# Where the wide operands of a 512-token encoder block lie within 512 bytes of a partition

## The chip, the cores and the metric

The kernel runs on one core of one Trainium2 chip. The metric is the device time of one execution in microseconds (us); lower is better. Before the change it took 1190.75 us, the median of three runs (1190.05 to 1191.32).

## The reference

One layer of a streaming encoder on `x` of 512 tokens by 1024 features, all in float32: a half-step SwiGLU feed-forward network, a mixer, a second half-step feed-forward network, a last RMS norm.

```python
x = x + 0.5 * swiglu(rms_norm(x, ffn1_norm), ffn1_w1, ffn1_w3, ffn1_w2)   # 1024 -> 2816 -> 1024
h = rms_norm(x, mix_norm)
p = h @ w_in                                     # 1024 -> 5288 columns, for all that follows
y_a = rwkv7_mixer(token_shift(p[..., :SHIFT_COLS]), ...) @ rwkv_proj      # 512 -> 1024
y_b = fox_mixer(p_fox, ...) @ fox_proj                                    # 512 -> 1024
x = x + (sigmoid(gate_a) * y_a + sigmoid(gate_b) * y_b) @ w_out           # 1024 -> 1024
x = x + 0.5 * swiglu(rms_norm(x, ffn2_norm), ffn2_w1, ffn2_w3, ffn2_w2)
out = rms_norm(x, final_norm)
```

`rwkv7_mixer` is a delta-rule recurrence over time with a 64 by 64 state for each of 8 heads; `fox_mixer` is causal attention with 8 heads and a cumulative forget bias.

## The kernel before, in words

**Tiles.** Activations are held with features on the 128 partitions and the 512 tokens along the partition, so a tile of one feature block is 128 x 512 float32, 2048 bytes of each partition. Weights come in slices of `kt` blocks of 128 rows by 128 columns, 512 bytes a block.

**Wide products.** Every product with a weight matrix is done by `mm3` (L123 to L126). Each operand is split into a high part, rounded to the matmul's `fp32r` format, and a low part with the rest; three matmuls add up `whi*xhi`, `whi*xlo` and `wlo*xhi` into one PSUM bank. One matmul loads a 128x128 stationary operand and streams a moving operand of 512 columns past it. In most stages the weight slice is stationary and the activation moves; in the value product of the attention (`pv`, L832) and in the last half of the second network's down projection (`po`, L1167) it is the other way round.

**Weights.** `load_raw` (L106) issues the DMA of a slice on SyncE's queue into one of three `raw` buffers. `split_w` (L113) makes `whi` by a cast on ScalarE and `wlo` by a subtraction on VectorE, two buffers of each. So a slice's DMA waits for a `raw` buffer, a cast for a `whi` buffer, and that for the matmuls that read it.

**Stages, in order of time.** The start (L245 to L385) transposes x and does the first pair of feed-forward products (`f`) from `fraw`, `fwhi`, `fwlo` and the normed `xh`, `xl`; its order on TensorE, VectorE and ScalarE is written out by hand. `ffn` (L446) does the up products `pa` and `pb` from `xh`, `xl`, makes `hh`, `hl` from them and does the down products `pd` from those. The mixer does `pl`, `pk`, `pgt`, `pq` and `pv` from `xh`, `xl` of the second norm. The recurrence (L879) and the attention (L945) run among gate products. Then come `ppj` (L1017), first with `yh`, `yl` and `fox_proj`, then with `ya` and `rwkv_proj`, and `pw` (L1107) from `mh`, `ml` with `w_out`. The second `ffn` follows; its columns of the upper half end in `last` (L1155) as `po`, and `out` is written.

**Order.** Outside the parts ordered by hand or held by `issue_after`, a planner with modelled times chooses each engine's order of instructions while the kernel is built.

**Layout.** A pool puts its tiles one behind another in the order in which the code first asks for them, each rounded up to 32 bytes. Pools opened later lie behind earlier ones, from the left end up, or from the right end down where they have `side="right"`. `cp` (constants, L61) is the first on the left and begins at byte 16512 of a partition, which is 128 past a multiple of 512; the right end is byte 229344, 480 past a multiple of 512. The pools on the left are `cp`, `xp` (`xh`, `xl`, `acc`, `rstd`), `wp` (`raw`, `whi`, `wlo`), `tp` (temporaries and the small `mx0`, `mx1`), then by stage `x0` (the start), `hp` (`hh`, `hl`) or `rp` (`nka`, `tiny`, `omu`, `rc`, `la`, `PC`, `V4`) and `sp` (`G`, `BK`, `RD`, `Tall`, whose places `mh`, `ya`, `codes`, `ml` take over). On the right are `xr1`, then `vtp` and `t2` (`vt`, `qk`, `khi`, `klc`, whose places `yh`, `yl` take over), then `xr2`.

Of the kernel before, what the change touches and what calls it, by code (L numbers as in the profile page):

```python
# [9 lines left out]
F32 = mybir.dt.float32  # L10
F32R = mybir.dt.float32r
BF16 = mybir.dt.bfloat16
AF = mybir.ActivationFunctionType
ALU = mybir.AluOpType
# [4 lines left out]
P = 128  # L19
# [6 lines left out]
NP = DA // P  # L26
# [9 lines left out]
PAR_W0, PAR_A0, PAR_KK, PAR_KA, PAR_RK, PAR_LG, PAR_LB = 38, 42, 46, 50, 54, 58, 62  # L36
# [14 lines left out]
def kernel(  # L51
# [7 lines left out]
    dve, act, pool, pe = nc.vector, nc.scalar, nc.gpsimd, nc.tensor  # L59

    cp = ctx.enter_context(tc.tile_pool(name="cp", bufs=1))  # L61
# [8 lines left out]
    def bank(name, pool_=None):  # L70
        pool_ = pool_ or pm
        return pool_.tile([P, T], F32, tag="b", name=name)

    def tmp(name, shape=(P, T), dt=F32, tag="t", **kw):
        return tp.tile(list(shape), dt, tag=tag, name=name, **kw)


    ident = cp.tile([P, P], F32, name="ident")
    make_identity(nc, ident)
    identb = cp.tile([P, P], BF16, name="identb")  # L80
    dve.tensor_copy(identb[:], ident[:])
    ones = cp.tile([P, P], F32, name="ones")
    dve.memset(ones[:], 1.0)
    onesr = cp.tile([P, P], F32R, name="onesr")
    dve.tensor_copy(onesr[:], ones[:])
    bones = cp.tile([P, P], F32, name="bones")
    dve.memset(bones[:], 0.0)
    dve.memset(bones[0:64, 0:64], 1.0)
    dve.memset(bones[64:128, 64:128], 1.0)
    center = cp.tile([P, P], F32, name="center")  # L90
    dve.scalar_tensor_tensor(center[:], bones[:], -1.0 / 64, ident[:], op0=ALU.mult, op1=ALU.add)
    bonesr = cp.tile([P, P], F32R, name="bonesr")
    dve.tensor_copy(bonesr[:], bones[:])
    epsr = cp.tile([P, 1], F32, name="epsr")
    dve.memset(epsr[:], RMS_EPS)
    epsl = cp.tile([P, 1], F32, name="epsl")
# [23 lines left out]
    def load_w(aps, kt, n, eng=None):  # L120
        return split_w(load_raw(aps, kt, n), kt, n, eng)

    def mm3(ps, whi, wlo, xhi, xlo, first, last):  # L123
        pe.matmul(ps, whi, xhi, start=first, stop=False)  # L124
        pe.matmul(ps, whi, xlo, start=False, stop=False)  # L125
        return pe.matmul(ps, wlo, xhi, start=False, stop=last)  # L126
# [14 lines left out]
    def split(dst_hi, dst_lo, src, hi_eng="act"):  # L141
        cast = act.copy(dst_hi, src) if hi_eng == "act" else dve.tensor_copy(dst_hi, src)
        dve.tensor_tensor(dst_lo, src, dst_hi.bitcast(F32), op=ALU.subtract)
        return cast
# [2 lines left out]
        return ap.bitcast(F32)  # L147


    xctx = ExitStack()  # L150
    rtp = xctx.enter_context(tc.tile_pool(name="xr1", bufs=1, side="right"))
    xT = [rtp.tile([P, T], F32, name=f"xT{c}") for c in range(KD)]
# [64 lines left out]
    par = cp.tile([P, PAR_N], F32, name="par")  # L217

    def pc(i):
        return par[:, i:i + 1]  # L220
# [3 lines left out]
    nc.scalar.dma_start(g1[:], ffn1_norm[0].rearrange("(a b) -> a b", b=P))  # L224
    warm = bank("warm", pf)
    for _ in range(5):
        pe.matmul(warm[:, 0:P], ones[:], ones[:], start=True, stop=True)
    gtp = bank("gtp", pr)
    pe.transpose(gtp[:, 0:8], g1[:], ident[0:8, 0:8])
    dve.tensor_copy(par[:, 0:8], gtp[:, 0:8])  # L230
# [12 lines left out]
            return call  # L243

    with tc.tile_pool(name="x0", bufs=1) as x0:  # L245
        qpe, qdve, qact = Queued(pe), Queued(dve), Queued(act)
        xin = [x0.tile([P, NB, P], F32, name=f"xin{c}") for c in range(KD)]
        fraw = [x0.tile([P, KD, P], F32, name=f"fraw{i}") for i in range(2)]
# [59 lines left out]

        def fill(n):
            for _ in range(n):  # L310
                qpe.matmul(warm[:, 0:P], ones[:], ones[:], start=True, stop=True)

        turn(0)
        x_hi(0)
# [131 lines left out]
    def ffn(nrm, w1, w3, w2, nxt, during=(), first=None, final=None):  # L446
        with tc.tile_pool(name="hp", bufs=1) as hp:
            hh, hl = [], []
            def hidden(j, pa, pb):
                a = tmp("fa")  # L450
                dve.tensor_tensor(a[:], pa[:], nrm.rstd[:], op=ALU.mult)  # L451
                sa = tmp("fs")
                act.activation(sa[:], a[:], AF.Silu)
                b = tmp("fb")
                dve.tensor_tensor(b[:], pb[:], nrm.rstd[:], op=ALU.mult)  # L455
                h = tmp("fh")
                dve.tensor_tensor(h[:], b[:], sa[:], op=ALU.mult)
                hi = hp.tile([P, T], F32R, name=f"hh{j}")
                lo = hp.tile([P, T], F32R, name=f"hl{j}")
                split(hi[:], lo[:], h[:], "dve")  # L460
                hh.append(hi)
                hl.append(lo)

            summed = None
            for j in range(KF):
                c0 = j * P
                if j == 0 and first:
                    continue
                pa = bank("pa", pf if j == 1 and first else pm)
                pb = bank("pb", pr)  # L470
                for ps, w in ((pa, w1), (pb, w3)):
                    if j == 1 and first:
                        wh, wl = first[1][ps is pb]
                    else:
                        wh, wl = load_w([(0, w[0][:, c0:c0 + P])], KD, P)
                    mms = nrm.cols(ps[:], wh, wl, P, [summed] if summed else [])
                    summed = None
                    if ps is pa and nrm.rstd is None:
                        if first is None:
                            nrm.parts()  # L480
                        summed = nrm.finish(mms[-1 if first is None else -2])
                        if first:
                            hidden(0, *first[0])
                if j in during:
                    with tc.issue_after(pin.ins), tc.issue_after(loads[-1].ins):
                        during[j]()
                hidden(j, pa, pb)
            cuts = ((0, 8), (8, 8), (16, 6))

            for m in range(KD // 2 if final else KD):  # L490
                ps = bank("pd")
                for k0, kn in cuts:
                    wh, wl = load_w([(0, w2[0][k0 * P:(k0 + kn) * P, m * P:(m + 1) * P])], kn, P)
                    for k in range(k0, k0 + kn):
                        mm3(ps[:], wh[:, k - k0, :], wl[:, k - k0, :], hh[k][:], hl[k][:], k == 0, k == KF - 1)
                dve.scalar_tensor_tensor(xT[m][:], ps[:], 0.5, xT[m][:], op0=ALU.mult, op1=ALU.add)
                nxt(m)
                if final and m == 1:
                    held = final[0]()
            if final:  # L500
                final[1](hh, hl, held)
# [4 lines left out]
    def mix_add(c):  # L506
        nc.gpsimd.dma_start(xsave[c], xT[c][:])
        mix.add(c)

    ffn(nrm, ffn1_w1, ffn1_w3, ffn1_w2, mix_add, {2: load_params, 4: masks, 10: place_params}, (first, second))  # L510

    W = w_in[0]
# [5 lines left out]
    with ExitStack() as mx:  # L518
        rp = mx.enter_context(tc.tile_pool(name="rp", bufs=1))
# [11 lines left out]
        spare = [h[:, i] for h in (duo("RD2", "spare0"), duo("RD3", "spare1")) for i in range(2)]  # L531
        Tall = sp.tile([P, 2 * C * C], F32, name="Tall", tag="Tall")

        nka = rp.tile([P, NP], F32, name="nka")
        dve.tensor_scalar(nka[:], par[:, PAR_KA:PAR_KA + NP], -1.0, None, op0=ALU.mult)
        tiny = rp.tile([P, 2], F32, name="tiny")
        dve.memset(tiny[:, 0:1], 1e-24)
        dve.memset(tiny[:, 1:2], -1e-24)
        omu = rp.tile([P, PAR_W0 - PAR_MU], F32, name="omu")
# [47 lines left out]
        for o, c0, mu in ((spare[2], DA, 4), (spare[3], 0, 0)):  # L587
            ps = bank("pk")
# [3 lines left out]
        for p in range(NP):  # L592
            za.append((zslots[2 * p], zslots[2 * p + 1]))
            for i, (w_, x_, par0, o) in enumerate(((uw, lw, PAR_W0, zslots[2 * p]), (ux, lx, PAR_A0, zslots[2 * p + 1]))):
                ps = bank("pz", (pr, pf)[i])
# [421 lines left out]
        def proj(m, wt, y):  # L1017
            wh, wl = load_w([(0, wt[0][:, m * P:(m + 1) * P])], NP, P)
            ps = bank("ppj")
            for k in range(NP):  # L1020
                mm3(ps[:], wh[:, k, :], wl[:, k, :], y[k][0], y[k][1], k == 0, k == NP - 1)
            return ps
# [18 lines left out]
        for p in range(NP):  # L1041
            y = vs[p]
            yc = bank("yc", pr)
            pe.matmul(yc[:], center[:], y, start=True, stop=True)
            sq = gslot[8 + p % 2]
            act.activation(sq, yc[:], AF.Square)
            ps = bank("pg", pf)
            pe.matmul(ps[:], bones[:], sq, start=True, stop=True)
            rn = tslot[p]
            with tc.issue_after(logs.ins):  # L1050
                act.activation(rn, ps[:], AF.Ln, bias=epsl[:, 0:1], scale=1.0 / 64)
                act.activation(rn, rn, AF.Exp, scale=-0.5)
            dve.tensor_tensor(y, yc[:], rn, op=ALU.mult)
            dve.scalar_tensor_tensor(y, y, pc(PAR_LG + p), bons[p], op0=ALU.mult, op1=ALU.add)
            ps = bank("pg", pf)
            pe.matmul(ps[:], gup[0:96, p * P:(p + 1) * P], lg[0:96, :], start=True, stop=True)
            dve.tensor_tensor(y, y, ps[:], op=ALU.mult)
            parted = split(*ya[p], y)
# [7 lines left out]
        for m in range(KD):  # L1066
            g = gslot[m]
            nc.gpsimd.dma_start(g, gsave[KD + m])
            ps = proj(m, fox_proj, ybs)
# [26 lines left out]
        for m in range(KD):  # L1096
            g = slot[m]
            ps = proj(m, rwkv_proj, ya)
# [4 lines left out]
        for m in range(KD):  # L1103
            wh, wl = load_w([(0, w_out[0][:, m * P:(m + 1) * P])], KD, P)
            ps = bank("pw")
# [49 lines left out]
    def last(hh, hl, ws):  # L1155
# [20 lines left out]
        for b in range(NB):  # L1176
# [11 lines left out]
            nc.sync.dma_start(out[0, bs, HC], hi_)  # L1188

    ffn(nrm2, ffn2_w1, ffn2_w3, ffn2_w2, almost, final=(hold, last))  # L1190


# [22 lines left out]
```

## Time and profile before

| | us |
|---|---|
| median of three runs | 1190.75 |
| span of the profiled execution, from its first to its last instruction | 1188.0 |
| TensorE busy with matmuls | 1173.7 |
| TensorE busy with weight loads | 946.0 |
| VectorE busy | 657.1 |
| ScalarE busy | 459.3 |
| GpSimd busy | 87.4 |

The profile is of one execution on the chip. Its span is 2.75 us under the median time; that difference lies outside the first and last instruction. A row of a group of instructions gives line, engine, operation, output and inputs, shape, count, busy time and the mean of one. A matmul's own duration holds the time that it takes to run through the array, and the next one starts before it has ended; what a stream of matmuls costs is read from the distance of their starts, and a busy TensorE is not one at its peak.

### The profile page before, as it was taken

To read this page: it belongs to the slowest core of one execution; us is meant where nothing else is said; L and a number is where in the kernel's file an instruction comes from. 1 tells how busy PE (TensorE), PEld (TensorE's weight loads), DVE (VectorE), ACT (ScalarE), POOL (GpSimd) and SP (SyncE) were. 2 spreads that over 40 slices of the span, in tenths; PEclk is the share of its full clock that TensorE was granted. 3 is DMA by queue.
4 is the path that set the end of the run, shared out by engine and by line. 5 is a ranking of instruction groups with operands and counts; after the bars stand their busy time and mean duration, and the time that the engine had idled before them with its cause. 6 is when DMAs were issued, how large, how long until landed. Compare 5 with 4: busy or idle time off the path is not lost.

```text
span 1188.0 us, 15711 instructions
## 1 busy us (share of the span) xinstructions
PE 1173.7 (99%) x6264; PEld 946.0 (80%) x6264; DVE 657.1 (55%) x983; ACT 459.3 (39%) x746; POOL 87.4 (7%) x138
## 2 busy tenths in 40 slices
PE   9999999999999999999999999999999999999997
PEld 7888888888887888887777776778888888888886
DVE  6645554533434697786767656766545454534221
ACT  6322222222223764346786765424222222223222
POOL 1200000001111111411000020121000000000100
PEclk9999999999999999999999999999999999999999
DMA  6333333333334243344122243633333333325211
GB/s 179 111 106 90 106 89 106 89 93 104 114 116 112 78 120 112 109 140 116 37 64 88 81 132 115 211 92 97 89 106 89 103 93 105 91 87 161 89 36 71
DMA packets 201783, 122.52 MB, mean 103 GB/s; under 512 B 9934, under 2 KB 191246, under 8 KB 201710
## 3 DMA queue, kind: packets, MB, share of 16 engines
q1 hardware_dynamic: 195134, 107.62, 31.1%
q0 software_dynamic: 3760, 12.06, 3.2%
q10 hardware_dynamic: 2816, 1.84, 0.5%
q8 instruction: 49, 0.80, 0.3%
q14 instruction: 24, 0.20, 0.1%
HBM read 110.82 MB, written 10.68 MB: 102 GB/s over the span
## 4 chain that ended last, share of the span: by engine, by line
PE 92%; DVE 3%; ACT 3%; DMA 1%; issue 1%; SPq 0%; ACTq 0%; DVEq 0%
PE pb L126 7%; PE pa L126 7%; PE pa L125 7%; PE pb L125 7%; PE pb L124 7%; PE pa L124 7%; PE pd L126 5%; PE pd L124 5%; PE pd L125 5%; PE pgt L124 3%; PE pgt L125 2%; PE pgt L126 2%; PE pk L124 2%; PE pk L125 2%; PE pk L126 2%; PE po L124 2%
## 5 line engine op out<-in xcount | busy, mean ns | idle before, releaser
L116 ACT CAST whi<-raw 128x1024 fp32r<-128x1024 f32 (+3 forms) x193 | 192.7, 999 | 592.0 <-PE pa L125 177.8
L117 DVE TENSOR_TENSOR wlo<-raw,whi 128x1024 fp32r<-128x1024 f32 (+3 forms) x193 | 224.3, 1162 | 125.1 <-ACT whi L116 125.0
L126 PE MATMUL pb<-xh,wlo 128*128 128x512 f32 x344 | 133.9, 389 | 0.0
L126 PE MATMUL pa<-xh,wlo 128*128 128x512 f32 x344 | 133.9, 389 | 0.0
L125 PE MATMUL pa<-xl,whi 128*128 128x512 f32 x344 | 133.9, 389 | 0.0
L124 PE MATMUL pb<-xh,whi 128*128 128x512 f32 x344 | 133.9, 389 | 0.0
L125 PE MATMUL pb<-xl,whi 128*128 128x512 f32 x344 | 133.9, 389 | 0.0
L124 PE MATMUL pa<-xh,whi 128*128 128x512 f32 x344 | 133.9, 389 | 0.0
L455 DVE TENSOR_TENSOR fb<-pb,rstd 128x512 f32<-128x512 f32 x43 | 29.7, 691 | 139.5 <-PE pb L126 139.5
L126 PE MATMUL pd<-hh,wlo 128*128 128x512 f32 x264 | 104.6, 396 | 0.0
L125 PE MATMUL pd<-hl,whi 128*128 128x512 f32 x264 | 104.2, 395 | 0.0
L124 PE MATMUL pd<-hh,whi 128*128 128x512 f32 x264 | 104.2, 395 | 0.0
L126 PEld LDWEIGHTS pb<-xh,wlo 128*128 128x128 f32 x344 | 64.5, 188 | 13.7 <-DVE wlo L241 0.5
L125 PEld LDWEIGHTS pb<-xl,whi 128*128 128x128 f32 x344 | 64.6, 188 | 13.5
L124 PEld LDWEIGHTS pb<-xh,whi 128*128 128x128 f32 x344 | 64.6, 188 | 13.5
L126 PEld LDWEIGHTS pa<-xh,wlo 128*128 128x128 f32 x344 | 64.6, 188 | 13.4
L125 PEld LDWEIGHTS pa<-xl,whi 128*128 128x128 f32 x344 | 64.5, 188 | 13.5
L124 PEld LDWEIGHTS pa<-xh,whi 128*128 128x128 f32 x344 | 64.6, 188 | 13.4
L451 DVE TENSOR_TENSOR fa<-pa,rstd 128x512 f32<-128x512 f32 x43 | 29.7, 691 | 70.2 <-PE pa L126 70.2
L126 PEld LDWEIGHTS pd<-hh,wlo 128*128 128x128 f32 x264 | 49.6, 188 | 12.3 <-DVE wlo L117 0.5
L125 PEld LDWEIGHTS pd<-hl,whi 128*128 128x128 f32 x264 | 49.6, 188 | 11.9
L124 PEld LDWEIGHTS pd<-hh,whi 128*128 128x128 f32 x264 | 49.6, 188 | 11.8
(397 smaller groups left out, 2031.1 us busy)
## 6 DMA issues: line engine op xcount, KB each, us to landing
raw<-in_ffn_w_dram SPq DMA_DIRECT2D x121, 512.0 KB
raw<-in_w_in_dram SPq DMA_DIRECT2D x40, 512.0 KB
raw<-in_ffn_w_dram SPq DMA_DIRECT2D x12, 384.0 KB
raw<-in_w_out_dram SPq DMA_DIRECT2D x8, 512.0 KB
gsave<-gs SPq DMA_DIRECT2D x9, 256.0 KB
xin<-in_x_dram SPq DMA_DIRECT2D x8, 256.0 KB
xsave<-xT POOLq DMA_DIRECT2D x8, 256.0 KB, 2.3
G<-gsave POOLq DMA_DIRECT2D x8, 256.0 KB, 3.0
```

The costliest lines, as they stand in the source:

```text
L116: (hi_eng or act).copy(hi[:], raw[:])
L117: (eng or dve).tensor_tensor(lo[:], raw[:], hi[:].bitcast(F32), op=ALU.subtract)
L124: pe.matmul(ps, whi, xhi, start=first, stop=False)
L125: pe.matmul(ps, whi, xlo, start=False, stop=False)
L126: return pe.matmul(ps, wlo, xhi, start=False, stop=last)
L451: dve.tensor_tensor(a[:], pa[:], nrm.rstd[:], op=ALU.mult)
L455: dve.tensor_tensor(b[:], pb[:], nrm.rstd[:], op=ALU.mult)
```

## The change

No instruction of the products is changed. Two constant matrices that were kept twice, once as float32 and once as `fp32r` (`ones`, `bones`), are kept once and read through either type, which takes 1024 bytes a partition and two casts away. Four unused or merged tiles shift what lies behind them: 192 bytes at the right end (`edge`), 384 bytes ahead of the start's tiles (`lead0`), 384 bytes ahead of `hh` and `hl` (`lead`), and `nka` and `tiny` in one tile in place of two, 32 bytes less.

```diff
-    ones = cp.tile([P, P], F32, name="ones")
-    dve.memset(ones[:], 1.0)
     onesr = cp.tile([P, P], F32R, name="onesr")
-    dve.tensor_copy(onesr[:], ones[:])
-    bones = cp.tile([P, P], F32, name="bones")
-    dve.memset(bones[:], 0.0)
+    ones = onesr[:].bitcast(F32)
+    dve.memset(ones, 1.0)
+    bonesr = cp.tile([P, P], F32R, name="bonesr")
+    bones = bonesr[:].bitcast(F32)
+    dve.memset(bones, 0.0)
     dve.memset(bones[0:64, 0:64], 1.0)
     dve.memset(bones[64:128, 64:128], 1.0)
     center = cp.tile([P, P], F32, name="center")
-    dve.scalar_tensor_tensor(center[:], bones[:], -1.0 / 64, ident[:], op0=ALU.mult, op1=ALU.add)
-    bonesr = cp.tile([P, P], F32R, name="bonesr")
-    dve.tensor_copy(bonesr[:], bones[:])
+    dve.scalar_tensor_tensor(center[:], bones, -1.0 / 64, ident[:], op0=ALU.mult, op1=ALU.add)
...
+    edge = ctx.enter_context(tc.tile_pool(name="edge", bufs=1, side="right"))
+    edge.tile([P, 48], F32, name="edge")
     xctx = ExitStack()
     rtp = xctx.enter_context(tc.tile_pool(name="xr1", bufs=1, side="right"))
...
     with tc.tile_pool(name="x0", bufs=1) as x0:
+        x0.tile([P, 96], F32, name="lead0")
...
         with tc.tile_pool(name="hp", bufs=1) as hp:
             hh, hl = [], []
+            hp.tile([P, 96], F32, name="lead")
+
...
-        nka = rp.tile([P, NP], F32, name="nka")
-        dve.tensor_scalar(nka[:], par[:, PAR_KA:PAR_KA + NP], -1.0, None, op0=ALU.mult)
-        tiny = rp.tile([P, 2], F32, name="tiny")
+        small = rp.tile([P, NP + 2], F32, name="small")
+        nka, tiny = small[:, 0:NP], small[:, NP:NP + 2]
+        dve.tensor_scalar(nka, par[:, PAR_KA:PAR_KA + NP], -1.0, None, op0=ALU.mult)
```

The other lines of the diff drop a `[:]` where `ones` and `bones` are used (L227, L311, L1048).

More of the change, by code (lines that the diff above doesn't have):

```diff
@@ L226 @@
     for _ in range(5):
-        pe.matmul(warm[:, 0:P], ones[:], ones[:], start=True, stop=True)
+        pe.matmul(warm[:, 0:P], ones, ones, start=True, stop=True)
     gtp = bank("gtp", pr)
@@ L310, in fill @@
             for _ in range(n):
-                qpe.matmul(warm[:, 0:P], ones[:], ones[:], start=True, stop=True)
+                qpe.matmul(warm[:, 0:P], ones, ones, start=True, stop=True)
         turn(0)
@@ L1047 @@
             ps = bank("pg", pf)
-            pe.matmul(ps[:], bones[:], sq, start=True, stop=True)
+            pe.matmul(ps[:], bones, sq, start=True, stop=True)
             rn = tslot[p]
```

## The prediction

> **What bounds the kernel now.** I read the profile's page first: busy times, the chain that ended last, then the groups.
>
> ```profile
> span 1188.0 us, 15711 instructions
> PE 1173.7 (99%) x6264; PEld 946.0 (80%) x6264; DVE 657.1 (55%) x983; ACT 459.3 (39%) x746; POOL 87.4 (7%) x138
> ...
> PEclk9999999999999999999999999999999999999999
> ...
> PE 92%; DVE 3%; ACT 3%; DMA 1%; issue 1%; SPq 0%; ACTq 0%; DVEq 0%
> ...
> L126 PE MATMUL pb<-xh,wlo 128*128 128x512 f32 x344 | 133.9, 389 | 0.0
> L126 PE MATMUL pd<-hh,wlo 128*128 128x512 f32 x264 | 104.6, 396 | 0.0
> ```
>
> TensorE is the bound: 92% of the chain is its matmuls, at a granted clock of 0.9 or more in every slice. So the time is the number of matmuls times the distance of their starts, and the groups hint that this is not the same everywhere: `pb` matmuls last 389 ns, `pd` matmuls of the same shape 396 ns. To get the distance itself I took stretches in which one product ran without a break. The columns are the stretch, its length, then busy time and count (x) for TensorE's matmuls and its weight loads, then other engines, granted clock, DMA share and GB/s. The first and fourth rows count every instruction, the others those of `pd`, `po` and `ppj` alone.
>
> ```profile
> 60.00:240.00 180.00, 180.00 (x796) 148.97 (x796) 89.55 (x116) 44.84 (x50) 0.00 (x0) 1.00 0.34 99
> ...
> 256.00:372.00 116.00, 116.00 (x499) 93.31 (x498) 4.84 (x7) 1.00 0.37 108
> ...
> 1132.00:1180.00 48.00, 48.00 (x208) 38.90 (x208) 2.08 (x3) 1.00 0.15 54
> ...
> 524.00:544.00 20.00, 20.00 (x90) 16.57 (x89) 16.66 (x37) 7.39 (x12) 2.60 (x7) 1.00 0.41 122
> ...
> 744.20:754.30 10.10, 10.10 (x45) 8.13 (x44) 2.20 (x4) 1.00 0.96 316
> ```
>
> A matmul under way at the left edge is counted too, so the distance is the length plus one duration (0.39 us), over the count. For `pa` and `pb` (first row) 180.39/796 = 226.6 ns; for `pq` (fourth) 20.39/90 = 226.6; for `pd` 116.39/499 = 233.3; for `po` 48.39/208 = 232.7; for `ppj` 10.49/45 = 233.1. For `pw` I use the first and the last of 28 rows in a stretch of the timeline (start, duration):
>
> ```profile
> 767.31 0.40 PE L124 MATMUL pw<-mh,whi 128*128 128x512 f32 x1
> ...
> 773.61 0.39 PE L124 MATMUL pw<-mh,whi 128*128 128x512 f32 x1
> ```
>
> That is 6.30/27 = 233.3 ns. All five rows show a clock of 1.00, and the DMA shares of `pa` (0.34) and `pd` (0.37) are alike, so neither explains 226.6 against 233.
>
> **What the layout says.** I worked out where each operand starts, mod 512 bytes, from the order and size of the declared tiles. `cp` starts at 128 and holds 4256 bytes, so `xp`, `wp` and the large temporaries lie at 288: `xh`, `xl`, `whi`, `wlo`. Behind them stand four 32-byte tiles (`mx0`, `mx1`), so `hh`, `hl` and the start's `fwhi`, `fwlo` lie at 416. In the mixer 160 bytes of small tiles, `la` (2048) and 256 of `PC` follow instead: 416+160+256 = 832, or 320, for `V4`, `ya`, `mh`, `ml`, `codes`. The right end and all of 2048 bytes under it lie at 480: `yh`, `yl`, `uw`, `ux`. So both operands of `pa`, `pb`, `pk`, `pgt`, `pq`, `pv` are at 288, and those are the products at 226.6 ns. The ones near 233 pair 416 with 288 (`pd`, and with the roles swapped `po`, `f`), 320 with 288 (`ppj`, `pw`), 480 with 288 (`ppj`). Neither a moving operand at 288 (`po` has it) nor a stationary one at 288 (`pd` has it) is enough; both have to agree.
>
> One product tests this apart from the stage and the region of memory. `pl` has `xh` and `whi` at 288 like `pk`, but its weight slice has 72 or 96 columns, so the blocks of a slice stand 288 or 384 bytes apart and most start elsewhere mod 512. First and last of 24 rows each:
>
> ```profile
> 374.48 0.39 PE L124 MATMUL pl<-xh,whi 128*72 128x512 f32 x1
> ...
> 379.80 0.39 PE L126 MATMUL pl<-xh,wlo 128*72 128x512 f32 x1
> ...
> 380.49 0.40 PE L124 MATMUL pl<-xh,whi 128*96 128x512 f32 x1
> ...
> 385.80 0.40 PE L126 MATMUL pl<-xh,wlo 128*96 128x512 f32 x1
> ```
>
> 5.32/23 = 231.3 ns and 5.31/23 = 230.9: not 226.6, though the weights are narrower. And the step comes at once where `pb` hands over to `pd`, with no wait between:
>
> ```profile
> 250.83 0.39 PE L125 MATMUL pb<-xl,whi 128*128 128x512 f32 x1
> 251.06 0.39 PE L126 MATMUL pb<-xh,wlo 128*128 128x512 f32 x1
> 251.29 0.40 PE L124 MATMUL pd<-hh,whi 128*128 128x512 f32 x1
> ```
>
> **The change, part by part.** *Addresses.* Two 512-byte constants go, 1024 bytes, which is 0 mod 512: `xh` and `whi` stay at 288. `lead` and `lead0` add 384: `hh`, `hl`, `fwhi`, `fwlo` go to 416+384 = 800, or 288. `small` saves 32: `V4` and all behind it go to 288. `edge` takes 192 off the right: `yh`, `yl` go to 288. So `f`, `pd`, `po`, `pw` and `ppj` all become 288 with 288. I take the 226.6 ns of the stretches that are so today. The counts are 3 matmuls for each block of weights:
>
> - `pd`: 3 x 264 = 792 matmuls by 233.3-226.6 = 6.7 ns: 5.31 us.
> - `po`: 4 token blocks x 22 x 3 = 264 by 6.1 ns: 1.61 us.
> - `pw`: 8 x 8 x 3 = 192 by 6.7 ns: 1.29 us.
> - `ppj`: 2 x 8 x 4 x 3 = 192 by 6.5 ns: 1.25 us.
> - `f`: 48. Eighteen of them took 4.20 us (below), 233.3 each; broken by transposes they may not all settle, so 0.15 to 0.32 us; I take 0.2.
>
> Sum 9.66 us. Now what of it is not collected. While `ppj` reads `ya` the DMA engines are 0.96 busy at 316 GB/s, and TensorE runs out of weights once:
>
> ```profile
> 744.97 10.01 DMA raw<-in_rwkv_proj_dram
> 755.08 0.63 ACT whi L116
> 755.75 0.50 PE ppj L124
> ...
> PE ppj L124 <- ACT whi L116: 1.0, 1, 1.0
> ```
>
> The slice was issued at 744.97, and its landing at 755 is set by the DMA engines, not by matmuls: the 48 between give 48 x 6.5 = 0.31 us that only lengthens this wait. In `pd` of the second network, where `hold` loads extra slices, a weight load waited 0.5 us for `wlo`; I take up to 0.3 us off there:
>
> ```profile
> PEld pd L126 <- DVE wlo L117: 0.5, 1, 0.5
> ACT whi L116 <- PE pd L125: 132.5, 34, 5.1
> ```
>
> The second row says that everywhere else in `pd` ScalarE waits for matmuls to free `whi`, 34 times, up to 5.1 us: weights stand ready, and `pa`, with the same 512 KB for 24 matmuls, is fed at 226.6 already. So 9.66-0.31-0.3 = 9.05 us, say 9.0.
>
> *Casts that go.* The start's chain, below, runs through SyncE's queue, a weight DMA, a cast and `f`; VectorE's two casts (0.72 and 0.23 us) lie before 2.7 us beside the 5.32 us DMA. They give nothing, and without that cover at most 0.95 us.
>
> ```profile
> 1.16 0.72 DVE L85 CAST onesr<-ones 128x128 fp32r<-128x128 f32 x1
> 2.44 0.23 DVE L93 CAST bonesr<-bones 128x128 fp32r<-128x128 f32 x1
> ...
> 1.86 5.32 DMA fraw<-in_ffn_w_dram
> 7.20 0.63 ACT fwhi L241
> 7.87 1.71 PE f L241 x6
> ...
> 17.78 4.20 PE f L241 x18
> ```
>
> *Merged `nka` and `tiny`.* The same three VectorE operations in the same order; no wait is added, no DMA and no queue. *Other pairs.* `pz` (8 matmuls, 320 with 480) becomes equal; `pn` (16: `khi` goes from 416 to 224 against `bonesr` at 384) and eight attention products against `qb0` (64 to 32, `klc` 480 to 288) stay unequal. At 6.7 ns either way, 32 matmuls are bounded by 0.2 us; I take 0. *VectorE, ScalarE and DMA* also read and write at moved places; the cast into `fwhi` at 416 took 0.63 us, that into `whi` at 288 the same 0.63 (rows above), so 0.
>
> The profiled span would be 1188.0-9.0 = 1179.0; 2.75 us outside it remain, so 1181.75.
>
> **The rivals.** *The offset is not the cause (no change).* The streams near 233 ns all have one operand above the temporaries, in the start's, the network's or the mixer's own pools, those at 226.6 have both below; the region could be it. Against it stands `pl`, both operands below and at 231. The time would be 1190.75. The Trainium skill speaks for this rival: "SBUF — State Buffer", section "Who interferes with whom", gives TensorE two independent read ports, one for the moving operand and one for weight loads, and says that TensorE never waits on anyone, by which the relative offset could cost nothing. The two distances above do not agree with it as far as it would mean one distance for all. That the padding lands elsewhere than I count belongs to this rival too. Chance 7%.
>
> *Only part settles.* Shift of phase, not the final place, makes the gain, and only unbroken streams keep it: `pd` of the first network (528) gains 3.5 us, the stages with waits, transposes or hand-overs half of their 5.5: 6.3 in all, 1184.5. If those gain nothing, 1187.2. For it: `pl` reads 231 even with some blocks equal. Against: `pq` shows 226.6 in a stretch with 37 VectorE instructions beside it. Chance 12%.
>
> *Slower: the planner re-orders the recurrence.* With two casts fewer its modelled times shift, and instruction order may change where no hand wrote it. The place is the recurrence, where TensorE was busy 162.49 of 167 us and waits on copies:
>
> ```profile
> 545.00:712.00 167.00, 162.49 (x1632) 125.26 (x1631) 114.05 (x244) 121.52 (x303) 8.75 (x16) 0.99 0.29 82
> 568.13 1.24 DVE wlo L117
> PE sps L901 <- ACT RD L896: 2.5, 3, 1.5
> ```
>
> A `wlo` subtraction (1.24 us) put ahead of the state update delays it and TensorE behind it. Over all 16 steps that is 19.8 us: 1190.75-9.0+19.8 = 1201.6. It decides from eight steps on (8 x 1.24 = 9.9). Against: the casts are over before 3 us, behind them stand hand-ordered operations, and SyncE's weights come later anyway. Chance 6%.
>
> **How the numbers follow.** Forecast 75%: 1181.75, its own range 1179.8 to 1183.5: below, nothing lost (9.66), the other pairs' 0.2, half of the casts' 0.95 and 0.6 for the spread of the runs; above, a loss three times as large and the same spread. Part settles 12%, no change 7%, slower 6%. To leave out no more than two in ten the range runs to 1185.5 and takes in half of the second case. About 0.2% (2.4 us) is what a measurement of this kernel can tell from no change: faster 0.87, same 0.07, slower 0.06.
>
> **What would show it.** In the changed profile `pd`, `po`, `pw`, `ppj` stand at about 389 ns a matmul and 226.6 from start to start, `pl` stays near 231, `pa` unchanged; `ppj` still waits once for weights near 745 to 755 less some 4 us, and its wait is 0.3 longer; the recurrence keeps its length. If the distances fall to 226.6 and the time does not, a wait has taken the gain: look in the stretch 700 to 780. If they stay at 233, the offset is not the cause.

## The result and the profile after

| | median us | runs | lowest to highest |
|---|---|---|---|
| before | 1190.40 | 4 | 1189.70 to 1191.32 |
| after | 1182.72 | 4 | 1181.52 to 1183.46 |

The ratio is 0.9935, with a 95% interval of 0.9923 to 0.9947: 6.3 to 9.2 us of 1190.4. The forecast was 1181.75. The profiled execution took 1182.64 us with a span of 1180.9, so that of the 9.05 us that the forecast took off the span 1188.0, 7.1 came.

The page of the changed kernel, the lines that answer to those of before (casts are now L114 and L115, `mm3` is L122 to L124):

```profile
span 1180.9 us, 15709 instructions
PE 1165.0 (99%) x6264; PEld 945.6 (80%) x6264; DVE 656.3 (56%) x981; ACT 459.5 (39%) x746; POOL 87.4 (7%) x138
...
PE 91%; ACT 3%; DVE 3%; DMA 2%; issue 1%; SPq 0%; ACTq 0%; DVEq 0%
...
L124 PE MATMUL pb<-xh,wlo 128*128 128x512 f32 x344 | 133.9, 389 | 0.1
...
L124 PE MATMUL pd<-hh,wlo 128*128 128x512 f32 x264 | 103.1, 391 | 0.5 <-DVE wlo L115 0.5
```

As many matmuls as before, and still the bound; those of `pd` now last 389 to 391 ns, no longer 396. The distances come from the same kind of stretch as before (stretch, length, then busy time and count of TensorE's matmuls, its weight loads and so on; the first and the last row count every instruction, the others those of `pd`, `po` and `ppj` alone):

```profile
60.00:240.00 180.00, 180.00 (x797) 148.96 (x796) 89.53 (x116) 44.84 (x50) 0.00 (x0) 1.00 0.34 98
...
256.00:368.00 112.00, 112.00 (x496) 92.75 (x495) 4.84 (x7) 1.00 0.39 112
...
1128.00:1174.00 46.00, 46.00 (x204) 37.91 (x202) 2.07 (x3) 1.00 0.13 46
...
740.50:750.30 9.80, 9.80 (x45) 8.10 (x44) 2.25 (x4) 1.00 0.96 322
...
545.00:712.00 167.00, 162.30 (x1628) 124.61 (x1627) 112.15 (x242) 122.27 (x303) 8.73 (x16) 0.99 0.29 84
```

`pa` and `pb` stay at 180.39/797 = 226.3 ns (226.6 before). `pd` has come down to 112.39/496 = 226.6 (from 233.3), `po` to 46.39/204 = 227.4 (from 232.7), `ppj` to 10.19/45 = 226.4 (from 233.1). TensorE's busy time in the recurrence's 167 us is 162.30 beside 162.49: nothing has moved there. Where `pb` hands over to `pd` the distance no longer rises. The three rows that the prediction shows of that place, 0.23 us apart on both sides, are too few to tell 226.6 from 233 ns at 0.01 us; the first and the 25th row of `pd` do tell them (timeline, start and duration; before, then changed):

```profile
251.29 0.40 PE L124 MATMUL pd<-hh,whi 128*128 128x512 f32 x1
...
256.88 0.40 PE L124 MATMUL pd<-hh,whi 128*128 128x512 f32 x1
```

```profile
251.33 0.39 PE L122 MATMUL pd<-hh,whi 128*128 128x512 f32 x1
...
256.77 0.39 PE L122 MATMUL pd<-hh,whi 128*128 128x512 f32 x1
```

That is 5.59/24 = 232.9 ns before and 5.44/24 = 226.7 now.

The one place that the forecast marked as a loser is the wait for the first slice of `rwkv_proj`. In the chain of waits of the changed kernel, and in the timeline of TensorE with the idle time in brackets:

```profile
741.32 10.47 DMA raw<-in_rwkv_proj_dram
751.88 0.63 ACT whi L114
752.55 0.50 PE ppj L122
...
750.47 0.39 PE L124 MATMUL ppj<-ya,wlo 128*128 128x512 f32 x1
752.55 0.50 PE L122 MATMUL ppj<-ya,whi 128*128 128x512 f32 x1 [1.69 <-ACT whi L114]
```

Before, the same wait was 1.0 us. The `ppj` matmuls from `ya` ahead of it gained 0.27 us, and the transfer took 10.47 us in place of 10.01: 0.27 + 0.46 is the whole of the longer wait (the gap between the two starts is 2.08 us, it was 1.36).

Where the 7.1 us arose is read from the starts of the stages' first and last matmuls in both timelines. The gain of a stage is the difference of its own length:

| stage | forecast us | measured us |
|---|---|---|
| start, up to the first `pa` (21.82 in both) and to the first `pd` | 0.2 | -0.04 |
| `pd` of the first network | 3.54 | 3.51 |
| up to `ppj`, with the recurrence | 0 | -0.13 |
| `ppj`, with its wait | 0.94 | 0.13 |
| `pw` | 1.29 | 1.17 |
| up products of the second network | 0 | 0.03 |
| `pd` of the second network, with its wait | 1.47 | 0.95 |
| `po` | 1.61 | 1.41 |
| sum | 9.05 | 7.03 |

The one long run of products without an interruption, `pd` of the first network, paid as worked out; the two stages with a wait for weights fell short, `ppj` by nearly all of its gain.

### The profile page after: what moved, and what is told of

It is laid out like the page before. It is cut to its first block, busy times and chain, and to the rows that moved or that the text cites. A ratio compares the mean times of both kernels' runs of the same rounds, so it can differ in the third digit from the quotient of the medians.

```text
span 1180.9 us, 15709 instructions
## 1 busy us (share of the span) xinstructions
PE 1165.0 (99%) x6264; PEld 945.6 (80%) x6264; DVE 656.3 (56%) x981; ACT 459.5 (39%) x746; POOL 87.4 (7%) x138
## 4 chain that ended last, share of the span: by engine, by line
PE 91%; ACT 3%; DVE 3%; DMA 2%; issue 1%; SPq 0%; ACTq 0%; DVEq 0%
PE pb L124 7%; PE pb L122 7%; PE pb L123 7%; PE pa L124 6%; PE pa L122 6%; PE pa L123 6%; PE pd L124 5%; PE pd L123 5%; PE pd L122 5%; PE pgt L122 3%; PE pgt L124 2%; PE pgt L123 2%; PE pk L123 2%; PE pk L122 2%; PE pk L124 2%; PE po L122 2%
## 5 line engine op out<-in xcount | busy, mean ns | idle before, releaser
L114 ACT CAST whi<-raw 128x1024 fp32r<-128x1024 f32 (+3 forms) x193 | 192.8, 1000 | 586.1 <-PE pa L123 177.8
L115 DVE TENSOR_TENSOR wlo<-raw,whi 128x1024 fp32r<-128x1024 f32 (+3 forms) x193 | 224.2, 1162 | 122.8 <-ACT whi L114 122.7
L124 PE MATMUL pb<-xh,wlo 128*128 128x512 f32 x344 | 133.9, 389 | 0.1
L124 PE MATMUL pa<-xh,wlo 128*128 128x512 f32 x344 | 133.9, 389 | 0.0
L122 PE MATMUL pb<-xh,whi 128*128 128x512 f32 x344 | 133.8, 389 | 0.0
L123 PE MATMUL pb<-xl,whi 128*128 128x512 f32 x344 | 133.8, 389 | 0.0
L123 PE MATMUL pa<-xl,whi 128*128 128x512 f32 x344 | 133.8, 389 | 0.0
L122 PE MATMUL pa<-xh,whi 128*128 128x512 f32 x344 | 133.8, 389 | 0.0
L124 PE MATMUL pd<-hh,wlo 128*128 128x512 f32 x264 | 103.1, 391 | 0.5 <-DVE wlo L115 0.5
L122 PE MATMUL pd<-hh,whi 128*128 128x512 f32 x264 | 102.8, 389 | 0.0
L123 PE MATMUL pd<-hl,whi 128*128 128x512 f32 x264 | 102.8, 389 | 0.0
L124 PEld LDWEIGHTS pb<-xh,wlo 128*128 128x128 f32 x344 | 64.5, 188 | 13.9 <-DVE wlo L241 0.6
L124 PEld LDWEIGHTS pa<-xh,wlo 128*128 128x128 f32 x344 | 64.6, 188 | 13.5
L123 PEld LDWEIGHTS pb<-xl,whi 128*128 128x128 f32 x344 | 64.6, 188 | 13.5
L123 PEld LDWEIGHTS pa<-xl,whi 128*128 128x128 f32 x344 | 64.5, 188 | 13.5
L122 PEld LDWEIGHTS pb<-xh,whi 128*128 128x128 f32 x344 | 64.6, 188 | 13.3
L122 PEld LDWEIGHTS pa<-xh,whi 128*128 128x128 f32 x344 | 64.6, 188 | 13.3
L124 PEld LDWEIGHTS pd<-hh,wlo 128*128 128x128 f32 x264 | 49.6, 188 | 11.1 <-DVE wlo L115 0.9
L123 PEld LDWEIGHTS pd<-hl,whi 128*128 128x128 f32 x264 | 49.6, 188 | 10.4
L122 PEld LDWEIGHTS pd<-hh,whi 128*128 128x128 f32 x264 | 49.6, 188 | 10.2
```

The lines of the kernel that those rows point to most:

```text
L114: (hi_eng or act).copy(hi[:], raw[:])
L115: (eng or dve).tensor_tensor(lo[:], raw[:], hi[:].bitcast(F32), op=ALU.subtract)
```

## The experiments

The theory: a 128x512 matmul starts 226.6 ns after the one ahead of it if both operands lie at one offset mod 512, and 233 if not, wherever they are. Its rivals: the gain comes from the casts or from another order of instructions; from the region or the absolute place; from a smaller condition than one offset mod 512. Every edit is against the changed kernel.

**Without the lead of `hh` and `hl`** (`pd` and `po` back at 416 with 288; the rest of the change stays).

```diff
             hh, hl = [], []
-            hp.tile([P, 96], F32, name="lead")
```

> The changed kernel without the 384 bytes ahead of hh and hl: these lie at 416 again, all other operands stay at 288. If the distance of the two operands mod 512 sets the pace, pd of both networks and po go back to about 233 ns from start to start and give back what they gained in the traces (3.5 + 0.9 + 1.4 us), so about 5.9 us more than the changed kernel, some 1188.6 us, with pw and ppj still at 226.6. If the region of memory, the dropped casts or the planner made the gain, the time stays at 1182.7.

Measured: 1188.92 us, ratio to before 0.9990 (0.9981 to 0.9999). Stretches of `pd` and of `po` in this kernel:

```profile
260.00:366.00 106.00, 106.00 (x456) 85.27 (x455) 4.84 (x7) 1.00 0.37 110
...
1130.00:1172.00 42.00, 42.00 (x183) 34.04 (x182) 1.51 (x3) 1.00 0.15 51
```

`pd` is at 106.39/456 = 233.3 ns again, `po` at 42.39/183 = 231.6. By the spans of the profiled executions (1186.9 beside 1180.9) some 6 of the 7 us hang on this one unused tile of 384 bytes.

**The constants alone** (`edge`, `lead0`, `lead` out, `nka` and `tiny` apart again; the two constant matrices stay merged).

```diff
-    edge.tile([P, 48], F32, name="edge")
...
-        x0.tile([P, 96], F32, name="lead0")
...
-            hp.tile([P, 96], F32, name="lead")
...
-        small = rp.tile([P, NP + 2], F32, name="small")
-        nka, tiny = small[:, 0:NP], small[:, NP:NP + 2]
...
+        nka = rp.tile([P, NP], F32, name="nka")
...
+        tiny = rp.tile([P, 2], F32, name="tiny")
```

> Only the constants are kept once; no padding, nka and tiny apart, so all operands have the offsets of the kernel before (1024 bytes less is 0 mod 512). Offset theory: the time of the kernel before, 1190.4, within 0.5 us, and every distance as before. If dropping two casts or the planner's new order helped, part of the 7.7 us appears here.

Measured: 1190.34 us, ratio 1.0003 (0.9994 to 1.0013). The casts that went and any shift of modelled times bring nothing that can be told; all of the gain lies in the places.

**Everything 32 bytes on** (all wide operands at 320).

```diff
+    cp.tile([P, 8], F32, name="shift")
...
-    edge.tile([P, 48], F32, name="edge")
+    edge.tile([P, 40], F32, name="edge")
```

> The changed kernel with everything moved on together by 32 bytes: all operands of the wide products at 320 in place of 288. If only their distance counts: 226.6 ns everywhere and 1182.7 us. If 288 itself is a good place, or a multiple of 64 or 128 a bad one: all 4500 wide matmuls near 233 ns, 20 us and more added.

Measured: 1182.69 us, ratio 0.9935 (0.9919 to 0.9952), as the changed kernel. The same stretch of `pd`:

```profile
260.00:366.00 106.00, 106.00 (x469) 87.76 (x468) 4.84 (x7) 1.00 0.39 114
```

106.39/469 = 226.8 ns. 288 is no special place; only the relation of the operands counts.

**128 bytes between `xp` and `wp`** (`xh`, `xl` stay at 288, the weights and all other wide operands go to 416). Now the products that were short in both kernels have unequal operands, and `pd`, `pw`, `ppj` equal ones. So has `po`, but for eight of its 22 blocks of weights (`ownh`, `ownl`): these are held in the places of `xh` and `xl`, at 288, and meet `hh`, `hl` at 416.

```diff
+    gap = ctx.enter_context(tc.tile_pool(name="gap", bufs=1))
+    gap.tile([P, 32], F32, name="gap")
...
-    edge.tile([P, 48], F32, name="edge")
+    edge.tile([P, 16], F32, name="edge")
```

> 128 bytes between the activations' pool and the weights' pool: xh and xl at 288, weights and all other operands at 416. Offset theory: pa and pb (2064 matmuls) go from 226.6 to about 233 ns, 13.8 us; pk, pgt, pq and pv (960) likewise where TensorE is the bound, 3 to 6.4 us; pd, po, pw and ppj stay at 226.6 because both of theirs are at 416. So 1199.5 to 1203 us. If both operands have to be at 288, pd, po, pw and ppj go back to 233 too: about 1208 to 1211. If the offsets do nothing: 1182.7.

Measured: 1200.53 us, ratio 1.0083 (1.0068 to 1.0098). First the stretch of `pa` and `pb`, then that of `pd`:

```profile
60.00:240.00 180.00, 180.00 (x775) 145.19 (x774) 87.67 (x114) 43.28 (x48) 0.00 (x0) 1.00 0.33 96
...
260.00:366.00 106.00, 106.00 (x470) 87.76 (x468) 4.84 (x7) 1.00 0.39 112
```

`pa` and `pb` now stand at 180.39/775 = 232.8 ns, `pd` at 106.39/470 = 226.4. Within `po` the eight blocks at 288 are long, 21 rows of which the first and last are

```profile
1158.69 0.40 PE L124 MATMUL po<-ownh,hh 128*128 128x512 f32 x1
...
1163.35 0.40 PE L126 MATMUL po<-ownh,hl 128*128 128x512 f32 x1
```

or 4.66/20 = 233.0 ns, while its steps with weights at 416 average 227.4. An unused 128 bytes cost 17.8 us against the changed kernel: `pa` and `pb` have 3 x 2 x 344 = 2064 matmuls and the mixer's products from `xh`, without `pl`, another 960 (40 slices of 24), at 6.2 ns each 18.7 us. This is the strongest evidence, since the effect was put where it had never been. It is also the test of the rule in the Trainium skill, page "SBUF — State Buffer", section "Who interferes with whom", that the moving operand and the weight loads have independent read ports and TensorE waits for nobody: as far as that would mean that their relative place costs nothing, this run does not agree.

**Small distances** (`hh` and `hl` 4 bytes from the weights in the first network, 16 in the second, `ya`, `mh`, `ml` 64, `yh`, `yl` 256).

```diff
+            hall = hp.tile([P, 2 * KF * T + 8], F32R, name="hall")
+            at = 4 if final else 1
...
-                hi = hp.tile([P, T], F32R, name=f"hh{j}")
-                lo = hp.tile([P, T], F32R, name=f"hl{j}")
+                hi, lo = [hall[:, at + i * T:at + (i + 1) * T] for i in (2 * j, 2 * j + 1)]
...
-        small = rp.tile([P, NP + 2], F32, name="small")
+        small = rp.tile([P, NP + 18], F32, name="small")
...
-    edge.tile([P, 48], F32, name="edge")
+    edge.tile([P, 112], F32, name="edge")
```

> The changed kernel with other distances between activation and weights, mod 512 bytes: 4 in pd of the first network, 16 in pd and po of the second, 64 in ppj with ya and in pw, 256 in ppj with yh; pa, pb and the mixer's input products stay equal. If the two have to agree to the byte: all these streams near 233 ns, pa at 226.6, and the time of the kernel before, 1189.5 to 1190.5 us. If only the coarse part of the address counts (lines of 32 or 64 bytes): pd and po keep 226.6 and some 5.9 us of the gain, about 1184.5 us.

**Large distances** (`hh`, `hl` 256 in the first network, -32 in the second, `ya`, `mh`, `ml` 96, `yh`, `yl` -64).

```diff
-            hp.tile([P, 96], F32, name="lead")
+            hp.tile([P, 88 if final else 160], F32, name="lead")
...
-        small = rp.tile([P, NP + 2], F32, name="small")
+        small = rp.tile([P, NP + 26], F32, name="small")
...
-    edge.tile([P, 48], F32, name="edge")
+    edge.tile([P, 64], F32, name="edge")
```

> As before with distances of 256 in pd of the first network, 32 less in pd and po of the second, 96 in ppj with ya and in pw, 64 less in ppj with yh. Agreement mod 512 needed: all near 233 ns and 1189.5 to 1190.5 us. If 256 is as good as 512: pd of the first network stays at 226.6 and keeps 3.5 us, about 1186.5 us. If one of these distances gives less than 226.6 ns, it would be a better place than the change's.

Measured: 1191.81 us, ratio 1.0012 (1.0003 to 1.0021), for the small ones; 1187.30, ratio 0.9975 (0.9964 to 0.9985), for the large ones. From the small distances, `pd` at 4 bytes, `po` at 16, `pw` at 64:

```profile
260.00:366.00 106.00, 106.00 (x447) 84.48 (x446) 4.85 (x7) 1.00 0.37 109
...
1130.00:1172.00 42.00, 42.00 (x182) 34.01 (x181) 1.38 (x2) 1.00 0.15 51
...
786.00:808.00 22.00, 22.00 (x98) 18.06 (x97) 2.77 (x4) 1.00 0.35 103
```

From the large ones, `pd` at 256, `po` at -32, `pw` at 96, and the first and last of 25 rows of `ppj` from `yh`, `yl` at -64:

```profile
256.00:368.00 112.00, 112.00 (x496) 92.75 (x495) 4.84 (x7) 1.00 0.39 112
...
1130.00:1172.00 42.00, 42.00 (x182) 33.74 (x181) 2.08 (x3) 1.00 0.13 47
...
786.00:808.00 22.00, 22.00 (x96) 17.69 (x95) 2.77 (x4) 1.00 0.33 97
...
733.64 0.40 PE L124 MATMUL ppj<-yh,wlo 128*128 128x512 f32 x1
...
739.24 0.40 PE L124 MATMUL ppj<-yh,wlo 128*128 128x512 f32 x1
```

| distance of activation from weights, bytes | ns from start to start |
|---|---|
| -64 (`ppj` from `yh`) | 5.60/24 = 233.3 |
| -32 (`po`) | 42.39/182 = 232.9 |
| 4 (`pd`) | 106.39/447 = 238.0 |
| 16 (`po`) | 42.39/182 = 232.9 |
| 64 (`pw`) | 22.39/98 = 228.5 |
| 96 (`pw`) | 22.39/96 = 233.2 |
| 128 (`pa`, `pb`) | 232.8 |
| 256 (`pd`) | 112.39/496 = 226.6 |

256 is as good as equal, in `yh` of the other kernel too, so the condition is weaker than the theory had it: equal mod 256. And 4 bytes is worse than 128: the 528 matmuls of `pd` at 238.0 rather than 233.3 are 2.5 us. That alone does not put the first of the two kernels over its expectation, since the profiled execution, which shows these distances, took 1190.50; its ten executions spread from 1190.40 to 1193.23, and no trace shows what the longer ones had. With 64 bytes the stream stood at 233.4 ns in `ppj` and, from the weight wait there, at 228.8, which it kept in `pw`; with -64 it did not come down. What decides between the two is open.

**One half of the hidden values apart.** In the first network `hh` equal and `hl` 128 bytes off, in the second the other way round: does one unequal operand upset all, or only its own step?

```diff
-            hp.tile([P, 96], F32, name="lead")
+            hp.tile([P, 128 if final else 96], F32, name="lead")
+            hall = hp.tile([P, 2 * KF * T + 96], F32R, name="hall")
+            at = KF * T + (96 if final else 32)
...
-                hi = hp.tile([P, T], F32R, name=f"hh{j}")
-                lo = hp.tile([P, T], F32R, name=f"hl{j}")
+                hi, lo = [hall[:, i + j * T:i + (j + 1) * T] for i in (0, at)]
```

> One of the two halves of the hidden activation apart from the weights by 128 bytes: in the first network hl (one matmul of three), in the second hh (two of three), the other half equal. If every matmul pays for its own distance: a third of 3.5 us and two thirds of 2.4 us come back, 1185.4 us, with a mean of 228.9 ns in pd of the first network. If a stream is either in step or not: both streams near 233 throughout and 5.9 us back, 1188.6 us.

Measured: 1185.36 us, ratio 0.9957 (0.9942 to 0.9972). Four matmuls of the first network's `pd`:

```profile
266.07 0.39 PE L122 MATMUL pd<-hall,whi 128*128 128x512 f32 x1
266.30 0.40 PE L123 MATMUL pd<-hall,whi 128*128 128x512 f32 x1
266.54 0.39 PE L124 MATMUL pd<-hall,wlo 128*128 128x512 f32 x1
266.76 0.39 PE L122 MATMUL pd<-hall,whi 128*128 128x512 f32 x1
```

The long step is the one behind L123, which moves `hl`; over the whole stretch the three steps average 226.7, 234.4 and 225.8 ns. So the price falls per matmul. But the total hides a mixed picture: in the second network `po` was long in all three steps (42.39/181 = 234.2 ns on average), although the third has equal operands, and `pd` there came to 229 where two long steps of three would give 231.

**`wlo` apart from `whi`.** `whi` and all moving operands at 288, `wlo` at 416. While one matmul runs, the next one's weights are loaded, as two rows of the kernel without the lead show, the matmul that reads `whi` and the load for the matmul behind it:

```profile
266.07 0.39 PE L122 MATMUL pd<-hh,whi 128*128 128x512 f32 x1
...
266.08 0.19 PEld L123 LDWEIGHTS pd<-hl,whi 128*128 128x128 f32 x1
```

So it can be asked whether a step's price goes by the matmul's own weights or by those loaded beside it.

```diff
-    loads = []
+    loads, gap = [], []
...
+        if not gap:
+            gap.append(wp.tile([P, 32], F32, tag="gap", name="gap", bufs=1))
...
-        x0.tile([P, 96], F32, name="lead0")
+        x0.tile([P, 64], F32, name="lead0")
...
-            hp.tile([P, 96], F32, name="lead")
+            hp.tile([P, 64], F32, name="lead")
...
-        small = rp.tile([P, NP + 2], F32, name="small")
+        small = rp.tile([P, NP + 98], F32, name="small")
```

> The changed kernel with only the low weight part wlo 128 bytes apart (416), everything else at 288. One in three of the wide matmuls has an unequal pair: whi*xh, whi*xl, wlo*xh. If a matmul pays for the distance between its own two operands, the long step of about 234 ns follows the start of the third (wlo). If it is the load of the next stationary operand, made while a moving operand streams, that has to agree with that moving operand, the long step follows the start of the second (whi*xl), while wlo is loaded. Either way one step in three is some 7.3 ns longer: 4500/3 x 7.3 = 11 us less what stalls hide, 1192 to 1194 us.

Measured: 1199.24 us, ratio 1.0062 (1.0045 to 1.0079), above both readings' 1192 to 1194. Four matmuls of `pb`:

```profile
232.06 0.40 PE L125 MATMUL pb<-xl,whi 128*128 128x512 f32 x1
232.29 0.40 PE L126 MATMUL pb<-xh,wlo 128*128 128x512 f32 x1
232.53 0.39 PE L124 MATMUL pb<-xh,whi 128*128 128x512 f32 x1
232.76 0.40 PE L125 MATMUL pb<-xl,whi 128*128 128x512 f32 x1
```

Over the stretch from 60 to 240 us the step behind `whi` with `xh` is 226.7 ns, behind `whi` with `xl` (own weights equal, the next ones apart) 232.5, behind `wlo` with `xh` (own apart, the next ones equal) 234.2. Each of the two readings had one long step of three, and the run has two. A step is short only when the moving operand agrees with its own weights and with the next ones. By that rule `po` in the experiment before has three long steps, as measured: its third matmul's next weights are `hh`, which is apart. And in this kernel's own `po`, where `whi` and `wlo` move and `hh` and `hl` are the weights, the rule gives one long step of three, the one that moves `wlo`; measured in the stretch

```profile
1145.00:1187.00 42.00, 42.00 (x186) 34.58 (x185) 2.08 (x3) 1.00 0.12 43
```

were 234.1 ns for the steps that move `wlo` and 226.7 and 225.9 for the two that move `whi`; where `ownh` and `ownl` move, which stay at 288, all three steps are at 226.5 to 226.8. The size of the total: two long steps of three in all 4512 wide matmuls but the 264 of `po`, at 693.4 rather than 680 ns for three, would cost 4248/3 x 13.4 = 19 us, and 16.5 was measured. Part of the difference lies in the gates among the recurrence (545 to 712 us), whose steps, broken into by other matmuls, average 231.1 ns in the changed kernel already and 231.6 here. `pd` of the second network in the experiment before stays 2 ns under the rule, without a reason.

**`pl` with its weight blocks equal.** The prediction leaned on `pl`, at 231, as a product with unequal operands. Here its weight blocks stand 512 bytes apart like all others (the constants are put in another order as well, so that `pn` has equal operands).

```diff
-        raw = wp.tile([P, kt, n], F32, tag="raw", name="raw", bufs=3)
+        raw = wp.tile([P, kt, max(n, P)], F32, tag="raw", name="raw", bufs=3)[:, :, 0:n]
...
-        hi = wp.tile([P, kt, n], F32R, tag="whi", name="whi", bufs=2)
-        lo = wp.tile([P, kt, n], F32R, tag="wlo", name="wlo", bufs=2)
+        hi, lo = [wp.tile([P, kt, max(n, P)], F32R, tag=f"w{t}", name=f"w{t}", bufs=2)[:, :, 0:n] for t in ("hi", "lo")]
...
```

> The changed kernel with the remaining unequal pairs made equal where that is easy: the blocks of pl's weights 512 bytes apart in place of 288 and 384, and onesr and bonesr at 288 like the operands that meet them. If offsets made pl differ from pk: pl goes from 231 to 226.6 ns, 48 x 4.4 ns = 0.2 us, with the few products of onesr and bonesr at most 0.3, so 1182.4 us, not to be told from 1182.7 by the time, only by the rows of pl. If the narrow weights made pl differ: it stays at 231.

Measured: 1182.44 us, ratio 0.9935 (0.9923 to 0.9948). First and last of the 24 rows with 72 columns:

```profile
371.24 0.40 PE L120 MATMUL pl<-xh,whi 128*72 128x512 f32 x1
...
376.55 0.40 PE L122 MATMUL pl<-xh,wlo 128*72 128x512 f32 x1
```

5.31/23 = 230.9 ns: equal offsets did nothing for `pl`.

**`pl` with 128 columns.** The same kernel, with the second half of `pl` on 128 columns in place of 96; it computes 32 columns more there, which nothing reads.

```diff
-        mix.cols(psg[0:96, :], *load_w(win(COL_G, 96), KD, 96), 96, [summed])
+        mix.cols(psg[:], *load_w(win(COL_G), KD, P), P, [summed])
```

> The kernel rest_equal with the second half of pl done on all 128 columns of its weight slice in place of 96 (the 32 more columns are the first gate's and are not used). If the narrow stationary operand makes pl slow: these 24 matmuls go from 230 to 226.7 ns, the first 24 (72 columns) stay at 230. If it is what runs beside them: both stay at 230.

Measured once: 1183.6 us. First and last of 24 rows, with 72 columns, then with 128:

```profile
370.48 0.40 PE L120 MATMUL pl<-xh,whi 128*72 128x512 f32 x1
...
375.79 0.40 PE L122 MATMUL pl<-xh,wlo 128*72 128x512 f32 x1
376.49 0.39 PE L120 MATMUL pl<-xh,whi 128*128 128x512 f32 x1
...
381.70 0.39 PE L122 MATMUL pl<-xh,wlo 128*128 128x512 f32 x1
```

5.31/23 = 230.9 ns beside 5.21/23 = 226.5. With offsets equal in both halves, `pl` is long where its weights are narrow and short where they are not.

## Why the prediction was right, and where it was not

**The cause and the price.** "Both have to agree" was right, and so were the two distances: 226.6 and 227.4 for `pd` and `po` in the changed kernel, 233.3 and 231.6 again when the lead alone was taken out, and 232.8 for `pa` and `pb` when 128 bytes were put between them and their weights. `pd` of the first network was forecast at 528 x 6.7 ns = 3.54 us and gave 3.51.

**The sum.** The forecast took 9.05 us off the span, and 7.1 came. Two fifths of the difference are `ppj`: 0.94 was forecast and 0.13 came. Of that, the wait grew by 0.72 rather than 0.31, because the transfer itself took 0.46 us longer, which the forecast held fixed; the part that reads `yh` gave 0.46 where 96 x 6.5 ns = 0.62 was counted, and 0.15 went at the hand-over to `ya`. Why the transfer takes longer was not tried; it took 10.24 us without the lead and 9.71 with the constants alone, but 10.27 with the small distances too, where `ppj` from `ya` was at 233. The wait of `pd` in the second network grew by 0.4 rather than up to 0.3 us (0.86 us from start to start in place of 0.44): its weight load waited 0.9 us for `wlo`, 0.5 before. At these two waits a shorter stream of matmuls ends early, the weights do not come earlier by as much, and TensorE waits.

**What the sum left out.** It gave 226.6 ns to every matmul of a stream. The rows of the changed kernel show that behind an interruption a stream does not stand there at once. In `pd` of the second network, behind the wait for `wlo`:

```profile
1080.82 0.40 PE L122 MATMUL pd<-hh,whi 128*128 128x512 f32 x1
...
1083.15 0.39 PE L123 MATMUL pd<-hl,whi 128*128 128x512 f32 x1
...
1085.19 0.40 PE L123 MATMUL pd<-hl,whi 128*128 128x512 f32 x1
```

The first ten steps take 2.33/10 = 233 ns each, the next nine 2.04/9 = 226.7. The other interruptions in `pd`, `po`, `pw` and `ppj` of this kernel look alike: two to ten steps that average 231 to 233 ns, then 226 to 227. That takes 0.01 to 0.06 us at each, and accounts for a part of what `yh`, `pw`, `po` and the second `pd` fell short by. The step `f`, counted at 0.2, gave nothing: `pa` begins at 21.82 in both kernels, right behind the last `f`. Transposes break `f` into pieces of six matmuls, too short to come down, and a last one of eighteen, which took 4.21 us up to `pa` in place of 4.28; 0.11 us went ahead of one set of transposes, for which no row shows a reason. Three rows of the last piece:

```profile
17.92 0.40 PE L241 MATMUL f<-xl,fwhi 128*128 128x512 f32 x1
...
20.46 0.39 PE L241 MATMUL f<-xh,fwhi 128*128 128x512 f32 x1
...
21.82 0.39 PE L122 MATMUL pa<-xh,whi 128*128 128x512 f32 x1
```

From 17.92 to 20.46 there are eleven steps of 231 ns, and only the last six, 1.36/6 = 226.7, are short. So the rival *only part settles* had seen something that is there; it charged half of the gain of these stages for it, and the rows show some hundredths of a us an interruption. The mechanism of the forecast was right, and the sizes of these terms were off.

**Luck in the total.** The forecast added 2.75 us outside the span. That was the median of three runs less the span of the profiled execution, which need not be the median one. Wherever the record has time and span of the same execution, they differ by 1.66 to 1.77 us, in the changed kernel by 1182.64 - 1180.9 = 1.74. With 1.74 the same sum would have said 1180.7, and its own range would have ended at 1182.5 in place of 1183.5. The error of 1.0 us hid half of the 2 us by which the gain was overrated, and so 1181.75 stands nearer to 1182.72 than the working deserved.

**The edits costed at nothing** were so: the two casts, the merged tile, `pn` and its like (1182.44 with `pn` equal beside 1182.72), and the planner's order. With this the rival that ended slower had no ground: the constants alone gave 1190.34, and the recurrence kept its length.

**The argument from `pl` was wrong.** It was to tell the offset from the region of memory, and it says nothing on either, since its narrow weights alone hold it at 231. What refutes the region is that `hh` and `hl`, in the same pool as before, fell to 226.6. The forecast survived because the other rows bore it: with `pl` struck out, the region should have had more than its 7%.

**"Mod 512" was too strict.** 256 is enough. For this change it makes no difference, since no pair before stood 256 apart.

**What stays open** is the mechanism. That two reads of one partition hinder each other when the addresses differ mod 256, one for the weights and one for the moving operand, would fit most rows, but no run shows the reads themselves, and the price of 4 bytes, the two distances seen at 64 bytes and the long steps behind an interruption are not explained by it.

## What to carry to other kernels

Where TensorE is the bound, measure the distance of matmul starts product by product; two values for one shape, here 226.6 and 233, are a hint to work out where the operands lie. Put a moving operand a multiple of 256 bytes from its stationary operand and from the next matmul's; an unused tile does it. Count the gain in full only for streams that nothing interrupts: behind an interruption the first steps, up to ten here, were long again.

## What the runs showed of the hardware that was not expected

- A distance of 256 bytes is as good as none, and the nearest miss is the dearest: 238.0 ns at 4 bytes, 232.9 at 16, 232.8 at 128, 226.6 at 256.
- A step depends on the moving operand beside two stationary ones, its own and the next: 226.7 where it agrees with both, 232.5 and 234.2 where it misses the one or the other.
- Equal operands do not bring the short step at once: behind an interruption two to ten steps averaged 231 to 233 ns before 226.6.
- A narrower stationary operand made the stream longer: 72 columns 230.9 ns, 128 columns 226.5, at the same spacing of the blocks, though a load of 72 columns is recorded at 140 ns and one of 128 at 188.
